# Pipelined gate eviction, an earlier first value slab, deeper look-ahead and row one-hots on two engines in a two-layer encoder

## The chip, the cores and the metric

The kernel runs on one core of a Trainium2 chip. The metric is the device time of one execution in microseconds (us). The engines are TensorE (PE, with its weight loads shown apart as PEld), VectorE (DVE), ScalarE (ACT), GpSimd (POOL) and SyncE (SP, which here only issues DMAs). Each engine takes its instructions strictly in the order of its own queue and waits on semaphores for the others.

## What is computed

Two layers, D = 1024, 256 tokens. Each layer is a mixer (a gated linear recurrence, then an RG-LRU block) followed by a product-key retrieval network over 16,384 experts, eight heads with sixteen experts each:

```python
scores = einsum('bshpd,hpkd->bshpk', q, sub_keys)
s1, i1 = top_k(scores[..., 0, :], 16);  s2, i2 = top_k(scores[..., 1, :], 16)
top_s, top_pos = top_k(s1 + s2 over all pairs, 16);  ids = i1 * 128 + i2 at top_pos
gate = softmax(top_s)
act = gelu(einsum('thkd,td->thk', u_tab[ids], h))
out = einsum('thk,thkd->td', gate * act, v_tab[ids])
```

The kernel computes the retrieval densely: every expert's activation for every token, times a 16,384 x 256 gate table that is zero where an expert was not chosen.

## The kernel before, in words

The change lies in `peer(i)` (line 1015) and its helpers; the mixers are as they were, apart from two helpers that they share. One `peer` has a query part, then two long stages.

**First stage** (64 calls of `s1`, line 1181). Slab g of `peer_u` (1 MB, 128 x 2048) is loaded by SP and taken in two half slabs. `split` (line 297) turns a half into a high and a low part: ACT copies it with rounding (line 300) into one of three buffers WS, DVE subtracts (line 301). `mm3` then runs 24 matmuls (lines 308, 309, 311). After a slab ACT takes the gelu of the result (line 1190) into the columns of A for that slab. `push` (line 279) keeps the splits `depth[0]` = 1 half slab ahead of the matmuls in program order; the buffer of a half is free again when the half three before it has been multiplied with its high part.

After every half slab `side(cost)` hands out credit to side work, which is written as generators that yield what they cost: first `routing` (top 16, softmax; credit 1.65 a half), then `gmats` (line 1192; credit 2.05 a half), which makes the gate table. It takes 32 blocks of eight tokens. `build` writes one-hot matrices on DVE: EQ of the second key index and P1, "row one-hots", of the first (both line 1204), and P2 = EQ times gate (line 1206). `mult(m)` runs four fp16 matmuls for half block m (line 1215) into two of six PSUM banks. `evict(m)` adds the high and low parts of the result: an ACT copy into the staging tile STG (line 1222, shown as xT, whose memory it uses), then a DVE add (line 1223). After a block's second half ACT issues the DMA of 512 KB that writes the block's gates to DRAM (line 1225). STG holds two blocks, so a block's first copy must wait until the DMA of the block two before it has landed.

**Second stage** (64 calls of `s2`, line 1258). For half slab j of `peer_v` a split as above; ACT copies and DVE subtracts the columns of A (lines 1296, 1297); 12 matmuls of 512 columns (line 1305) accumulate into four PSUM banks. Before A is used it is multiplied by the gates, read back from DRAM in 16 slabs of 1 MB (`gd`): `gates` (line 1245) does one DVE product of 128 x 2048 for each (line 1252), two of them right after each other for every eight value slabs. Layer 0 also reduces 24 slabs of `w_ada` here (`ada_slab`, line 394), each as two DVE instructions, after a broadcast (`row_bcast`, lines 374 and 375) of the condition; `softplus` too is side work of this stage. In layer 1 `pre_final` is.

`order` is the list of all weight slabs in the order of use. `pump` issues the next one as soon as a slot of the arena is free, and stops at a `gd` slab until the gate table is written (`tabled`). In the second half of the first stage three slots are left; the second stage gets three more at value slab 18.

Of the kernel before, what the change touches and what calls it, by code (L numbers as in the profile page):

```python
# [16 lines left out]
AF = mybir.ActivationFunctionType  # L17
# [3 lines left out]
P = 128  # L21
# [21 lines left out]
ADA_TE = 2  # L43
GLEAD = 2
GS16 = 32768.0
C_ROUTE = 1.65
C_G0 = 2.05
C_G1 = 1.45

SM = {}  # L50
# [22 lines left out]
def body(ctx, tc, A, out):  # L73
# [218 lines left out]
    def flush():  # L292
        while queue:
            run_one()
        run_posts(0)

    def split(raw):
        n = wsn[0] % NWS
        wsn[0] += 1
        ACT.activation(WS[:, n, 0], raw, AF.Copy)  # L300
        V.tensor_tensor(WS[:, n, 1], raw, WS[:, n, 0], op=OP.subtract)  # L301
        return WS[:, n, 0], WS[:, n, 1]

    def mm3(o, ws, rs, ks, start=True, stop=True):
        wh, wl = ws
# [64 lines left out]

    def row_bcast(cols, bank):

        for k in range(KD):
            V.tensor_scalar(diag[:, k % 2], ident, cols[:, k:k + 1], float(D), op0=OP.mult, op1=OP.mult)
            PE.matmul(PS[:, bank + k // 4, k % 4 * P:(k % 4 + 1) * P], ones, diag[:, k % 2], start=True, stop=True)
            if k % 2:
                yield 0.8

    cs = pool.tile([P, KD], F32, name="cond")

# [4 lines left out]
        yield from row_bcast(cs, bank)  # L385
        cond_copy(bank)

    def ada_slab():
        n, raw = take("ada")
        i, s = order[n][1:]  # L390
        for m in range(2):
            col = 2 * s + m
            r_ = raw[:, m * 1024:(m + 1) * 1024]
            V.scalar_tensor_tensor(r_, r_, 1.0, cb, op0=OP.mult, op1=OP.mult, accum_out=mod[:, i, col:col + 1])  # L394
        free(n)
        if s % 4 == 3:
            c0 = 2 * (s - 3)
            V.tensor_tensor(mod[:, i, c0:c0 + 8], mod[:, i, c0:c0 + 8],
                            sv("b_ada")[:, i * 48 + c0:i * 48 + c0 + 8], op=OP.add)
            if c0 == 40:  # L400

                V.tensor_scalar(mod[:, i, c0:c0 + 8], mod[:, i, c0:c0 + 8], 1.0 / GS16, None, op0=OP.mult)

    def weaved():
        while st["taken"] < len(order) and order[st["taken"]][0] == "ada":
            ada_slab()

    epst = pool.tile([P, 2], F32, name="eps")
    V.memset(epst, EPS)
# [604 lines left out]
    def peer(i):  # L1014
# [179 lines left out]
        def gmats():  # L1194

            P2 = pool.tile([P, 2, NTB, 2, P], F16, name="gsplit", tag="gsplit")

            def build(n):
                bf = n % 2
                ts = slice(n * NTB, (n + 1) * NTB)  # L1200
                pairs = lambda a: a.rearrange("p t (j z) -> p t j z", z=2)
                spread = lambda a: a[:, ts, None, :].to_broadcast([P, NTB, P // 2, 2])
                for dst, t_ in ((EQ, T2), (P1[:, bf], T1)):
# [13 lines left out]

            def evict(m):
                b = 2 + 2 * (m % 3)
                pv = PS[:, b:b + 2].rearrange("p a (t g j) -> p g j (a t)", t=2, g=2)  # L1220
                st_ = STG[:, m // 2 % 2, :, m % 2 * 4:m % 2 * 4 + 4]
                ACT.activation(st_, pv[:, 0], AF.Copy)  # L1222
                V.tensor_tensor(st_, pv[:, 1], st_, op=OP.add)  # L1223
                if m % 2:
                    nc.scalar.dma_start(Gd[i][:, :, m // 2],
                                        STG[:, m // 2 % 2].rearrange("p (q j) t -> p q (j t)", q=8))
# [12 lines left out]
            yield 1.0  # L1239
            for m in (S // 4 - 2, S // 4 - 1):  # L1240
                evict(m)
                yield 0.7
            tabled.add(i)
            pump()

        def gates():

            n, raw = take("gd")
            q, th = order[n][2] // 2, order[n][2] % 2
            av = slabs(aslab(16 * q), 2).rearrange("p a (j t) -> p (a j) t", t=S)[:, :, th * P:(th + 1) * P].rearrange(  # L1250
                "p j (g t) -> p j g t", t=8)
            V.tensor_tensor(av, av, raw.rearrange("p (g j t) -> p j g t", g=16, t=8), op=OP.mult)  # L1252
            free(n)

        box_wt = []
        wtn = [0]
# [1 line left out]
        def s2(cost):  # L1258
            n, raw = take("v")
            g = order[n][2]  # L1260
            if g == 63 and i == 1:
                boxes = []

# [20 lines left out]
            for half in range(2):  # L1284
# [3 lines left out]
                def prep(half=half, j=j, box=box):  # L1288
                    hi, lo = split(raw[:, half * 1024:(half + 1) * 1024])
                    if half == 1:  # L1290
                        free(n)
                    z = wtn[0] % 4
                    wtn[0] += 1
                    box["v"] = (hi, lo)
# [31 lines left out]
        if i == 0:  # L1326
            sides.append(cond)
            sides.append(softplus())
        for it in vs[i]:
            if it[0] == "ada":  # L1330
                settle(cond)
                weaved()
                continue
            if it[0] == "gd":
                gates()
                continue
            g = it[2]
            if g == 4:
                nc.sync.dma_start(XT, Xd[i])
            elif g == 18:  # L1340
                release(0, 1, 2)
            elif g == 34 and i == 0:
                release(3, 4, 5, 6, 7)
            elif g == 52 and i == 0:
                reserve(0, 1, 2, 3, 4, 5, 6)
            elif g == 58 and i == 0:
                release(13)
            s2(C_G1)
            if g == 63 and i == 1:
                flush()  # L1350
            if i == 1 and g == 44:
                sides.append(pre_final())
        if i == 0:
            release(17, 18)

# [154 lines left out]
```

## Time and profile before

| | before |
|---|---|
| median of 3 runs (range) | 2033.39 us (2030.5 to 2035.17) |
| profiled execution: its time, its span | 2030.43 us, 2028.6 us |
| mean granted TensorE clock, share of full speed | 0.986 |
| PE, PEld, DVE, ACT busy | 1943.8, 1781.8, 1571.2, 1004.0 us |
| chain that ended last | PE 88%, DVE 6%, ACT 3%, DMA 2%, issue 1% |
| HBM read and written | 418 and 37 MB |

The profile is one execution taken by the hardware profiler. A busy PE is not PE at its peak, since matmuls overlap. The chain that ended last is followed back from the last instruction, at each step to what released it. The first stage runs from about 288 to 692 us in layer 0 and from about 1244 to 1647 us in layer 1, the second from there to 1070 and to 2015 us.

### The profile page before, as it was taken

Reading aid. Unit: us, or ns where it says so; the run is one execution under the profiler, and the core shown is the slowest. Engines: PE = TensorE matmul, PEld = TensorE weight load, DVE = VectorE, ACT = ScalarE, POOL = GpSimd, SP = SyncE. Lnnn points to the kernel's source line nnn. Section 1 sums busy time; section 2 is a strip of 40 time slices with the busy share of each in tenths; the row PEclk is TensorE's granted clock in tenths of the full one; section 3 lists DMA queues with packets and bytes.
Section 4 is the critical chain, followed back from the end, with each engine's and each line's share of the span. In section 5 each row is a group of like instructions: output and inputs, shape, how many; then the busy total and the mean of one; then the engine's idle time right before and its main releaser. Section 6 shows DMA issues by size and latency. Waiting matters only on the chain.

```text
span 2028.6 us, 32101 instructions
## 1 busy us (share of the span) xinstructions
PE 1943.8 (96%) x12862; PEld 1781.8 (88%) x12862; DVE 1571.2 (77%) x2797; ACT 1004.0 (49%) x1419; POOL 0.2 (0%) x4
## 2 busy tenths in 40 slices
PE   6999999999999799999999989999999979999998
PEld 6898899999999777888888889999999978888786
DVE  6798659887888677888877776988788866676575
ACT  3544544445555354444445744445455544454454
POOL 0000000000000000000000000000000000000000
PEclk9999999999999899999999999999999989999999
DMA  8654714455767667989753482545676766766561
GB/s 347 271 200 163 285 69 158 175 187 198 238 193 244 210 247 269 394 347 399 290 208 154 158 306 90 185 167 192 208 244 195 235 225 261 290 252 260 203 234 57
DMA packets 125765, 456.87 MB, mean 225 GB/s; under 512 B 7720, under 2 KB 73512, under 8 KB 74672
## 3 DMA queue, kind: packets, MB, share of 16 engines
q1 hardware_dynamic: 59056, 421.28, 55.4%
q10 hardware_dynamic: 66560, 33.56, 5.5%
q8 instruction: 100, 1.64, 0.3%
q14 instruction: 49, 0.40, 0.1%
HBM read 418.10 MB, written 36.70 MB: 224 GB/s over the span
## 4 chain that ended last, share of the span: by engine, by line
PE 88%; DVE 6%; ACT 3%; DMA 2%; issue 1%; SPq 0%; DVEq 0%; ACTq 0%
PE psum L1305 33%; PE psum L311 14%; PE psum L308 14%; PE psum L309 14%; PE psum L1215 3%; PE psum L478 2%; DVE wsplit L301 1%; PE psum L358 1%; DMA arena<-peer_v_dram 1%; PE psum L688 1%; PE psum L318 1%; PE psum L595 1%; ACT wsplit L300 1%; PE psum L1088 1%; PE psum L915 1%
## 5 line engine op out<-in xcount | busy, mean ns | idle before, releaser
L301 DVE TENSOR_TENSOR wsplit<-arena,wsplit 128x1024 fp32r<-128x1024 f32 x600 | 729.7, 1219 | 300.8 <-ACT wsplit L300 298.4
L300 ACT ACTIVATE wsplit<-arena 128x1024 fp32r<-128x1024 f32 x600 | 632.4, 1056 | 492.1 <-PE psum L1305 311.4
L1305 PE MATMUL psum<-wsplit,gsplit 128*128 128x512 f32 x3048 | 703.3, 392 | 19.4 <-ACT gsplit L1296 14.3
L1305 PEld LDWEIGHTS psum<-wsplit,gsplit 128*128 128x128 f32 x3048 | 574.8, 189 | 145.3 <-ACT gsplit L1296 15.4
L308 PE MATMUL psum<-hsplit,wsplit 128*128 128x256 f32 x2448 | 607.7, 286 | 2.1 <-ACT wsplit L300 2.1
L309 PE MATMUL psum<-hsplit,wsplit 128*128 128x256 f32 x2448 | 600.5, 283 | 0.0
L308 PEld LDWEIGHTS psum<-hsplit,wsplit 128*128 128x128 f32 x2448 | 469.1, 192 | 4.3 <-ACT wsplit L300 2.7
L309 PEld LDWEIGHTS psum<-hsplit,wsplit 128*128 128x128 f32 x2448 | 469.6, 192 | 0.1
L311 PE MATMUL psum<-hsplit,wsplit 128*128 128x256 f32 x2448 | 344.2, 283 | 2.7 <-DVE wsplit L301 2.7
L311 PEld LDWEIGHTS psum<-hsplit,wsplit 128*128 128x128 f32 x2448 | 316.5, 192 | 3.1 <-DVE wsplit L301 3.1
L1190 ACT ACTIVATE arena<-psum 128x512 f32<-128x512 f32 x128 | 76.5, 598 | 283.2 <-PE psum L311 283.2
L1223 DVE TENSOR_TENSOR xT<-psum,xT 128x512 f32<-128x512 f32 x128 | 87.6, 686 | 51.9 <-ACT xT L1222 51.9
L1297 DVE TENSOR_TENSOR gsplit<-arena,gsplit 128x256 fp32r<-128x256 f32 x254 | 105.9, 417 | 0.0
L1296 ACT ACTIVATE gsplit<-arena 128x256 fp32r<-128x256 f32 x254 | 101.4, 399 | 0.0
L394 DVE SCALAR_TENSOR_TENSOR arena<-arena,scratch 128x1024 f32<-128x1024 f32 x80 | 94.1, 1218 | 0.0
L1252 DVE TENSOR_TENSOR arena<-arena 128x2048 f32<-128x2048 f32 x32 | 71.9, 2284 | 12.2 <-DMA arena<-gates 12.2
L1222 ACT ACTIVATE xT<-psum 128x512 f32<-128x512 f32 x128 | 75.1, 589 | 8.1 <-PE psum L1215 8.1
L1206 DVE TENSOR_TENSOR gsplit<-scratch 128x2048 f16<-128x2048 f16 x64 | 78.0, 1218 | 0.0
L1215 PE MATMUL psum<-gsplit,scratch 128*128 128x256 f16 x512 | 67.0, 274 | 0.0
L1215 PEld LDWEIGHTS <-scratch 128*128 128x128 f16 x512 | 44.9, 98 | 7.1
L697 DVE TENSOR_TENSOR arena<-arena 128x512 f32<-128x512 f32 x56 | 35.7, 683 | 12.0 <-PE psum L688 6.8
L1204 DVE TENSOR_TENSOR scratch<-iota,T 128x1024 f16<-128x1024 f16 x64 | 43.8, 684 | 0.0
(219 smaller groups left out, 1258.5 us busy)
## 6 DMA issues: line engine op xcount, KB each, us to landing
arena<-peer_u_dram SPq DMA_DIRECT2D x128, 1024.0 KB, 4.9
arena<-peer_v_dram SPq DMA_DIRECT2D x128, 1024.0 KB, 4.9
arena<-w_ada_dram SPq DMA_DIRECT2D x40, 1024.0 KB, 5.9
gates<-xT ACTq DMA_DIRECT2D x64, 512.0 KB, 5.3
arena<-gates SPq DMA_DIRECT2D x32, 1024.0 KB, 4.7
arena<-w_q_dram SPq DMA_DIRECT2D x16, 1024.0 KB, 6.9
arena<-hg_k_dram SPq DMA_DIRECT2D x8, 1024.0 KB, 15.5
arena<-hg_s_dram SPq DMA_DIRECT2D x8, 1024.0 KB, 6.1
```

Of the source, the lines that this page charges most:

```text
L300: ACT.activation(WS[:, n, 0], raw, AF.Copy)
L301: V.tensor_tensor(WS[:, n, 1], raw, WS[:, n, 0], op=OP.subtract)
L308: PE.matmul(o, wh(k), rh(k), start=start and k == 0, stop=False)
L309: PE.matmul(o, wh(k), rl(k), start=False, stop=False)
L311: PE.matmul(o, wl(k), rh(k), start=False, stop=stop and k == ks - 1)
L394: V.scalar_tensor_tensor(r_, r_, 1.0, cb, op0=OP.mult, op1=OP.mult, accum_out=mod[:, i, col:col + 1])
L1206: V.tensor_tensor(P2[:, bf].rearrange("p t g (j z) -> p t g j z", z=2), pairs(EQ)[:, :, None].to_broadcast([P, NTB, 2, P // 2, 2]), TG[:, ...
L1215: PE.matmul(PS[:, b + t // 2, t % 2 * S:(t % 2 + 1) * S], P1[:, n % 2, 4 * h + t], P2[:, n % 2, 4 * h + t], start=True, stop=True)
L1223: V.tensor_tensor(st_, pv[:, 1], st_, op=OP.add)
L1296: ACT.activation(box_wt[0][:, z, 0], acol(j), AF.Copy)
L1297: V.tensor_tensor(box_wt[0][:, z, 1], acol(j), box_wt[0][:, z, 0], op=OP.subtract)
L1305: PE.matmul(PS[:, 4 + 2 * tb + dh], box_wt[0][:, z, a, tb * P:(tb + 1) * P], r[:, dh * 512:(dh + 1) * 512], start=(j == 0 and a == 0 and r ...
```

## The change

1. `evict` becomes `step(m)`, one per half block. It issues the DMA of a finished block (half block m-3 is its second), then the ACT copy of half block m-1, the DVE add of m-2, and the matmuls of m.
2. In 11 of the 32 blocks (n % 3 == 1) ACT makes the row one-hots: eight Abs of 128 x 128 with a bias column, then one Relu over 128 x 1024; DVE then makes only EQ and P2.
3. The credit of a half slab rises (1.65 to 1.7, 2.05 to 2.2); a block yields 2.7 + 0.7 + 0.7 as before, or 2.0 + 0.7 + 0.7 where ACT makes its one-hots.
4. In the second stage the splits run two half slabs ahead (`depth[0] = 2`), with five buffers: H, idle there, lends two (`widen`). Value slab 0 stands ahead of the first two gate slabs in `order`.
5. The gate products are cut into quarters of a pair (128 x 1024) and handed out one per half slab (`between`), as are the halves of an `ada` slab. Arena slots are released one by one from value slab 5 on; the broadcast of the condition starts at slab 4, softplus at slab 20.

```diff
-C_ROUTE = 1.65
-C_G0 = 2.05
+C_ROUTE = 1.7
+C_G0 = 2.2
...
-                    if max(0, 8 * q - GLEAD) == it[2]:
+                    if q and 8 * q - GLEAD == it[2]:
                         zs += [("gd", i, 2 * q), ("gd", i, 2 * q + 1)]
             zs.append(it)
+            if it[0] == "v" and it[2] == 0:
+                zs += [("gd", i, 0), ("gd", i, 1)]
...
     def split(raw):
-        n = wsn[0] % NWS
+        hs = homes[-1]
+        w_ = hs[wsn[0] % len(hs)]
...
+    def between():
+        for xs in (steps_gate, steps_ada):
+            if xs:
+                xs.pop(0)()
+                return
...
+            def by_act(n):
+                return n % 3 == 1
+
+            def row_onehots(n, part):
+
+                if not by_act(n) or n >= S // NTB:
+                    return
+                if part == 2:
+                    ACT.activation(P1[:, n % 2], P1[:, n % 2], AF.Relu, scale=-1.0, bias=1.0)
+                    return
+                for t in range(4 * part, 4 * part + 4):
+                    ACT.activation(P1[:, n % 2, t], io1, AF.Abs, scale=-1.0, bias=T1[:, n * NTB + t, 0:1])
...
-            def evict(m):
-                b = 2 + 2 * (m % 3)
...
-                ACT.activation(st_, pv[:, 0], AF.Copy)
-                V.tensor_tensor(st_, pv[:, 1], st_, op=OP.add)
-                if m % 2:
-                    nc.scalar.dma_start(Gd[i][:, :, m // 2],
...
+            def step(m):
+
+                if m - 3 >= 0 and (m - 3) % 2:
+                    n = (m - 3) // 2
+                    nc.scalar.dma_start(Gd[i][:, :, n], STG[:, n % 2].rearrange("p (q j) t -> p q (j t)", q=8))
+                if 0 <= m - 1 < S // 4:
+                    pv, st_ = view(m - 1)
+                    ACT.activation(st_, pv[:, 0], AF.Copy)
+                if 0 <= m - 2 < S // 4:
+                    pv, st_ = view(m - 2)
+                    V.tensor_tensor(st_, pv[:, 1], st_, op=OP.add)
+                if m < S // 4:
+                    mult(m)
 
             for n in range(S // NTB):
                 build(n)
-                yield 2.7
-                if n:
-                    evict(2 * n - 2)
-                    yield 0.7
-                mult(2 * n)
-                if n:
-                    evict(2 * n - 1)
-                    yield 0.7
-                mult(2 * n + 1)
...
+                row_onehots(n + 1, 0)
+                yield 2.0 if by_act(n) else 2.7
+                step(2 * n)
+                row_onehots(n + 1, 1)
                 yield 0.7
+                step(2 * n + 1)
+                row_onehots(n + 1, 2)
+                yield 0.7
...
+            for z in range(2):
+                for th in range(2):
+                    steps_gate.append(lambda z=z, th=th: part(z, th))
...
+        depth[0] = 2
+        widen([H[:, n].rearrange("p k t -> p (k t)").rearrange("p (a x) -> p a x", a=2) for n in range(2)])
```

Two places show how rows move. The first is ACT's queue in layer 0's first stage, with the semaphores that a row waits for (DMAHW is a DMA's). Before, around one block (L1190 gelu, L1222 copy of a half block, L1225 the block's DMA, L300 split):

```order
L1222 ACTIVATE xT<-psum 128x128x4
L1225 DMA gates<-xT 1024x1x128 [waits DVE_49]
L300 ACTIVATE wsplit<-arena 128x1024 [waits DMAHW1_49,Activation_49]
L1222 ACTIVATE xT<-psum 128x128x4 [waits DMAHW5_49,PE_49]
L300 ACTIVATE wsplit<-arena 128x1024 [waits Activation_49]
L1190 ACTIVATE arena<-psum 128x512 [waits PE_49]
```

Now, around one block (L1225 is now the gelu, L1275 the block's DMA, L1278 the copy, L317 the split):

```order
L1275 DMA gates<-xT 1024x1x128 [waits DVE_49]
L1278 ACTIVATE xT<-psum 128x128x4 [waits PE_49]
L1278 ACTIVATE xT<-psum 128x128x4 [waits DMAHW0_49,PE_49]
L317 ACTIVATE wsplit<-arena 128x1024
L1225 ACTIVATE arena<-psum 128x512
L317 ACTIVATE wsplit<-arena 128x1024 [waits DMAHW2_49,Activation_49]
```

In both, the copy that waits for a DMA writes the staging buffer of the block two before its own. Before, that block's DMA stands one block further up in the queue: the DMA shown in the fence is the next one. Now `step(2N)` issues the DMA of block N-2, and `step(2N+1)` brings the copy of half block 2N that waits for it: the DMA is the one shown, one copy above.

The second place is DVE's queue where layer 0's second stage begins. Before (L301 split, L1223 add, L1252 gate product, L1297 A's low part, L374 broadcast):

```order
L301 TENSOR_TENSOR wsplit<-arena,wsplit 128x1024
L1223 TENSOR_TENSOR xT<-psum,xT 128x128x4 x3
L1252 TENSOR_TENSOR arena<-arena 128x16x128 x2
L301 TENSOR_TENSOR wsplit<-arena,wsplit 128x1024
L1297 TENSOR_TENSOR gsplit<-arena,gsplit 128x256
L374 TENSOR_SCALAR scratch<-consts,cond 128x128 x6
```

Now (L318 split, L1281 add, L1310 quarter product, L1366 A's low part):

```order
L1281 TENSOR_TENSOR xT<-psum,xT 128x128x4 x2
L318 TENSOR_TENSOR wsplit<-arena,wsplit 128x1024 x10
L1310 TENSOR_TENSOR arena<-arena 128x8x128 x2
L1366 TENSOR_TENSOR gsplit<-arena,gsplit 128x256
L318 TENSOR_TENSOR wsplit<-arena,wsplit 128x1024
L1310 TENSOR_TENSOR arena<-arena 128x8x128
```

Before, the last adds of the gate table stand right ahead of the first gate products; now ten splits lie between them, and the broadcast has left this place.

## Rows read from the trace of the kernel before

**Rows 1.** The page: PE busy in tenths, 40 slices of the span.
```profile
PE   6999999999999799999999989999999979999998
```

**Rows 2.** Stretches of 20 us: busy PE, PEld, DVE, ACT, POOL; clock, DMA share, GB/s.
```profile
300.00:320.00 20.00, 20.00 (x169) 20.00 (x168) 20.00 (x90) 8.26 (x10) 0.00 (x0) 1.00 0.38 137
...
600.00:620.00 20.00, 20.00 (x171) 19.63 (x170) 17.69 (x22) 10.84 (x16) 0.00 (x0) 1.00 0.73 238
...
680.00:700.00 20.00, 12.46 (x106) 12.01 (x104) 10.66 (x12) 4.99 (x8) 0.00 (x0) 0.87 0.49 161
700.00:720.00 20.00, 13.71 (x56) 10.61 (x56) 11.01 (x26) 10.85 (x17) 0.00 (x0) 0.79 0.46 182
...
920.00:940.00 20.00, 19.06 (x85) 15.41 (x84) 18.45 (x24) 9.26 (x15) 0.00 (x0) 1.00 1.01 422
...
1640.00:1660.00 20.00, 9.10 (x68) 8.52 (x68) 9.68 (x10) 5.00 (x9) 0.00 (x0) 0.76 0.62 229
```

**Rows 3.** Chain of work that ended last, pieces: start us, us, what.
```profile
249.70 0.96 PE psum L311 x8
252.58 0.96 PE psum L311 x8
...
688.71 0.47 PE psum L1215 x4
...
689.83 1.30 DVE xT L1223 x2
691.15 3.47 DMA gates<-xT
...
695.17 6.69 DMA arena<-peer_v_dram
```

**Rows 4.** Timeline of ACT in layer 0's first stage: start us, us, instruction, idle before.
```profile
559.83 0.60 ACT L1190 ACTIVATE arena<-psum 128x512 f32<-128x512 f32 x1 [1.68 <-PE psum L311]
560.33 0.59 ACT L1222 ACTIVATE xT<-psum 128x512 f32<-128x512 f32 x1
561.67 0.52 ACTq L1225 DMA_DIRECT2D gates<-xT  x1
562.30 1.06 ACT L300 ACTIVATE wsplit<-arena 128x1024 fp32r<-128x1024 f32 x1 [1.38 <-DVE scratch L1204]
563.26 0.58 ACT L1222 ACTIVATE xT<-psum 128x512 f32<-128x512 f32 x1
563.74 1.05 ACT L300 ACTIVATE wsplit<-arena 128x1024 fp32r<-128x1024 f32 x1
...
568.31 0.52 ACTq L1225 DMA_DIRECT2D gates<-xT  x1
```

**Rows 5.** The chain of work that ended last, later pieces.
```profile
882.52 42.95 PE psum L1305 x188
...
1016.87 53.16 PE psum L1305 x233
...
1643.94 0.47 PE psum L1215 x4
...
2015.01 1.37 PE psum L1278 x6
```

**Rows 6.** Groups of instructions: count, busy us and mean ns, idle before.
```profile
L1296 ACT ACTIVATE gsplit<-arena 128x256 fp32r<-128x256 f32 x254 | 101.4, 399 | 0.0
...
L1252 DVE TENSOR_TENSOR arena<-arena 128x2048 f32<-128x2048 f32 x32 | 71.9, 2284 | 12.2 <-DMA arena<-gates 12.2
...
L926 ACT ACTIVATE arena<-psum,smalls 128x256 f32<-128x256 f32 x32 | 13.0, 476 | 2.8 <-PE psum L915 2.8
```

**Rows 7.** DMA issues: count, size each, median us to landing.
```profile
arena<-gates SPq DMA_DIRECT2D x32, 1024.0 KB, 4.7
```

**Rows 8.** Line 1225 from 500 to 685 us: the gate write's issue to its landing.
```profile
DMA to landing us min/median/max: 3.5/5.3/6.8
```

More of the change, by code (lines that the diff above doesn't have):

```diff
@@ L295, in flush, with widen, narrow @@
         run_posts(0)
+    homes = [[WS[:, n] for n in range(NWS)]]
+    kept = []
+    def widen(more):
+        n = wsn[0]
+        homes.append([homes[0][(n + z) % NWS] for z in range(NWS)] + more)
+        kept.append(n)
+        wsn[0] = 0
+    def narrow():
+        homes.pop()
+        wsn[0] = kept.pop()
     def split(raw):
-        n = wsn[0] % NWS
+        hs = homes[-1]
+        w_ = hs[wsn[0] % len(hs)]
         wsn[0] += 1
-        ACT.activation(WS[:, n, 0], raw, AF.Copy)
-        V.tensor_tensor(WS[:, n, 1], raw, WS[:, n, 0], op=OP.subtract)
-        return WS[:, n, 0], WS[:, n, 1]
+        ACT.activation(w_[:, 0], raw, AF.Copy)
+        V.tensor_tensor(w_[:, 1], raw, w_[:, 0], op=OP.subtract)
+        return w_[:, 0], w_[:, 1]
     def mm3(o, ws, rs, ks, start=True, stop=True):
@@ L371, in row_bcast @@
     def row_bcast(cols, bank):
[L373 to L377, printed above, removed]
+        for k in range(0, KD, 2):
+            for z in range(2):
+                V.tensor_scalar(diag[:, z], ident, cols[:, k + z:k + z + 1], float(D), op0=OP.mult, op1=OP.mult)
+            yield 0.8
+            for z in range(2):
+                PE.matmul(PS[:, bank + k // 4, (k + z) % 4 * P:((k + z) % 4 + 1) * P], ones, diag[:, z], start=True,
+                          stop=True)
+            yield 0.1
     cs = pool.tile([P, KD], F32, name="cond")
@@ L386, in load_cond, with ada_parts, ada_part @@
         cond_copy(bank)
-    def ada_slab():
+    def ada_parts():
         n, raw = take("ada")
+        return [lambda m=m: ada_part(n, raw, m) for m in range(2)]
+    def ada_part(n, raw, m):
         i, s = order[n][1:]
[L391 to L394, printed above, removed]
+        col = 2 * s + m
+        r_ = raw[:, m * 1024:(m + 1) * 1024]
+        V.scalar_tensor_tensor(r_, r_, 1.0, cb, op0=OP.mult, op1=OP.mult, accum_out=mod[:, i, col:col + 1])
+        if m == 0:
+            return
         free(n)
@@ L405, in weaved @@
         while st["taken"] < len(order) and order[st["taken"]][0] == "ada":
-            ada_slab()
+            for f in ada_parts():
+                f()
+    steps_ada, steps_gate = [], []
+    def between():
[3 more added lines that the diff above has]
+                return
     epst = pool.tile([P, 2], F32, name="eps")
@@ L1246, in gates, with part @@
         def gates():
[L1248 to L1253, printed above, removed]
+            two = [take("gd"), take("gd")]
+            def part(z, th):
+                n, raw = two[th]
+                q = order[n][2] // 2
+                av = slab(aslab(16 * q + 8 * z)).rearrange("p (j t) -> p j t", t=S)[:, :, th * P:(th + 1) * P].rearrange(
+                    "p j (g t) -> p j g t", t=8)
+                V.tensor_tensor(av, av, raw.rearrange("p (g j t) -> p j g t", g=16, t=8)[:, 8 * z:8 * z + 8], op=OP.mult)
+                if z == 1:
+                    free(n)
+            for z in range(2):
+                for th in range(2):
+                    steps_gate.append(lambda z=z, th=th: part(z, th))
         box_wt = []
@@ L1260, in s2 @@
             g = order[n][2]
+            while g % 8 == 0 and g and steps_gate:
+                steps_gate.pop(0)()
             if g == 63 and i == 1:
@@ L1291, in prep @@
                         free(n)
+                    if j == 0:
+                        gates()
+                        between()
+                    between()
                     z = wtn[0] % 4
@@ L1339, in peer @@
                 nc.sync.dma_start(XT, Xd[i])
[L1340 to L1344, printed above, removed]
+                if i == 0:
+                    sides.append(cond)
+            if g == 20 and i == 0:
+                sides.append(softplus())
+            if g % 4 == 1 and g > 4:
+                z = g // 4 - 1
+                if z in ((0, 1, 2, 3, 4, 5, 6, 7) if i == 0 else (0, 1, 2, 7)):
+                    release(z)
+            if g == 52 and i == 0:
                 reserve(0, 1, 2, 3, 4, 5, 6)
@@ L1347, in peer @@
                 release(13)
+            if g == 63:
+                depth[0] = 1
             s2(C_G1)
@@ L1352, in peer @@
                 sides.append(pre_final())
+        narrow()
+        while steps_ada:
+            steps_ada.pop(0)()
         if i == 0:
```

25 lines of the change are left out of this document (12 added, 13 removed).

## The prediction, made before the change was run

> **What bounds the kernel now.** I read the page first, then the table of 20 us stretches, the chain that ended last, and the timelines of ACT and DVE. The page's slices show PE busy almost everywhere, with dips at the ends of the stages [rows 1]. In the first stage PE never stops: 20.00 of 20 us at full clock, with DVE at 17.69 and ACT at 10.84 [rows 2]. So nothing that only frees DVE there can save time; it can only cost. A half slab takes PE 2.88 us, the distance of two groups of eight low-part matmuls [rows 3], and a block of eight fp16 matmuls 6.64 - 2 x 2.88 = 0.88 us, where 6.64 us is the distance of two gate writes [rows 4].
>
> The time that can be won lies in the second stage. In layer 0 the last fp16 matmul ends at 689.18 us [rows 3], one half slab of 2.88 us follows it, and the second stage ends at 1070.03 us [rows 5]: 378.0 us. Its 1524 matmuls at 42.95/188 = 0.2285 us are 348.2 us [rows 5]. That leaves 29.8 us. Layer 1's, counted the same way, runs from 1647.29 to 2015.01 us: 367.7 us, 19.5 us over [rows 5]. The chain says what the gap at the start is: last add, gate write 3.47 us, then value slab 0 behind two gate slabs, 6.69 us [rows 3]. The clock falls there too, to 0.87 and 0.79 of full speed, 0.76 in layer 1 [rows 2]. A smaller, repeated loss is the pair of gate products, 2 x 2.28 us of DVE at once [rows 6], after which PE misses 0.94 us in a stretch [rows 2].
>
> **The second stage: a gain.** The credits now end the gate table about ten half slabs before the first stage does (counted in the built order of PE's queue: the last fp16 group stands 11 half slabs before the first matmul of the second stage; before, one). The write and the wait for it thus lie beside 29 us of matmuls, and value slab 0 no longer queues behind the gate slabs. The gate product in quarters costs DVE the same sum, some 1.14 us a time, beside matmuls; two half slabs of look-ahead cover that. The condition's broadcast and layer 1's transposes stay on PE: 48 small matmuls, by four in 0.47 us [rows 3] up to twice as long, 6 to 11 us. Of 29.8 + 19.5 = 49.3 us at most some 41 can go. Something stays at the start: the arena has three slots there, the second gate slab waits for the last `peer_u` slab's slot, needs 4.7 us to land [rows 7] and two quarter products before value half 0 can be multiplied. I put this at 6 us a layer, clock included, an estimate. **Gain: 41 - 12 = 29 us**, between 8 (little more than the 0.94 us gaps, of which there are five) and 41.
>
> **The first stage: a new wait on ACT.** Taking 11 one-hots of 128 x 1024 from DVE, and its wait for the ACT copy, gains nothing: PE is full there. What the eviction as a pipeline adds decides. Before, a block's first copy waits for a gate write that was issued more than a block earlier, over 6.64 us, against 5.3 us to land (3.5 to 6.8) [rows 4, 8]: the wait is over when ACT gets there. Now that write is issued one copy ahead of the copy that waits for it. ACT works in order, so it stands until the write has landed, and all splits queue behind it. With three WS buffers ACT cannot be far ahead of PE: a buffer is free when two thirds of the half slab three before are done, and the split takes 1.06 us [rows 4], so its lead is at most 2 x 2.88 + 0.96 - 1.06 = 5.7 us; I take 5.
>
> In the built order of layer 0 there are 30 such waits. Between a waiting copy and the next gate write, ACT's queue holds in all 30 copies, 42 splits, 21 gelus, 40 Abs and 10 Relu; only the rest (30 copies, 10 splits, 5 gelus, 40 Abs) lies beside a landing. From start to start a copy takes 0.48, a split 0.96, a gelu 0.50 us [rows 4]; a Relu of the split's size 0.96. An Abs does not occur before: 0.399 us for 256 columns [rows 6] less 0.10 for 128 of them (512 take 0.60 [rows 4]), plus 0.08 for a bias column (0.476 against 0.399 [rows 6], the nearest row), less the 0.10 by which neighbours overlap: 0.28, between 0.20 and 0.38. The sum is 14.4 + 40.3 + 10.5 + 11.2 + 9.6 = 86.0 us. ACT's queue therefore needs 30 L + 86.0 us, where L is the time from issue to landing. In the same stretch PE needs 52 half slabs and 30 blocks: 52 x 2.88 + 30 x 0.88 = 176.2 us. What ACT needs more, less its lead, is a stall of PE.
>
> L is 3.5 us with nothing beside it [rows 3, 8] and 5.3 us at the median, where a `peer_u` slab is in flight. Now 26 slabs fall on the 30 writes, and a slab is issued when its second split is done, close to the next write, sometimes just behind it. I take 4.7, nearer to 5.3. Then ACT needs 227.0 us, 50.8 more than PE, and **a layer loses 45.8 us, two layers 92 us**. At 3.5 it is 9.8 us a layer, 20 in all; at 5.3 it is 63.8, 128 in all.
>
> The trace's 3.5 us for 512 KB on idle DMA engines is the floor of L. [...]
>
> The rest is costed at nothing. Splitting eight fp16 matmuls into four and four: the blocks' period shows no price for the change of type beyond the 0.88 us. The higher routing credit: DVE is full in the routing's bursts, 20.00 of 20, with PE also at 20.00 [rows 2]; 0.05 more credit over some 60 half slabs is about 3 us of work moved forward, cover enough if spread, up to 3 us a layer if not. DVE's waits behind ACT are hidden as long as ACT is the later of the two. XT's reload at value slab 4 stays where it was. ACT's queue still carries the gate writes' issue, 0.52 us, within L.
>
> **Sum.** +92 - 29 = +63 us on the profiled execution's 2030.4 us, 2093; its runs' median is 3.0 us above it, so 2033.4 + 63 = **2096 us**. A measurement of this kernel can tell about 0.2%, 4 us, from no change.
>
> **Rivals.**
> 1. *The landing is short (faster).* The writes land as if alone, because PE's and so the slabs' pace falls and they seldom meet. For it: 3.5 us does occur. Against: 26 slabs for 30 writes, and 5.3 at the median with the same mix. At 3.5 us: +20 - 29 gives 2024 us; without any stall 2004 us. The point from which it decides: 2 x (30 L + 86.0 - 176.2 - 5) = 29, L = 3.66 us. Chance 0.14. [...]
> 2. *The landing is a little above that.* L from 3.66 to 4.1 us gives 0 to +27 us, 2033 to 2060 us. [...] Chance 0.12, a third of it within 0.2%.
> 3. *The writes collide fully.* In the slowed rhythm slab and write are issued at the same moment, in every block, and L is 6 us (6.8 occurs [rows 8]): +170 - 29, 2174 us. PE's many short stops could lower its clock as well, as in the stretches at 0.79 and 0.87 [rows 2]; against that, 920 to 940 us has a stop and a clock of 1.00. Chance 0.12.
> 4. *The second stage's gain stays out*, because DVE, at 18.45 of 20 us in layer 0 [rows 2], cannot run ahead: then, with layer 0's 20 us lost, +83 instead of +63, 2116 us. This lies inside the forecast's range.
>
> **How the numbers follow.** The forecast, L between 4.1 and 5.5 us, has 0.62: 55.6 to 139.6 us of stalls, with the gain of 29 2060 to 2144 us, and some 10 us more on either side for the gain's own bounds. Rivals 1, 2 and 3 have 0.14, 0.12 and 0.12. Faster is rival 1; the same is a third of rival 2, 0.04; slower is the rest, 0.82. The range that leaves out 2 in 10 goes from 2022 us (half of rival 1 lies below it) to 2155 us (rival 3 lies above it).
>
> **What would show it.** Right: in the first stages PE below 16 of 20 us while the gate table is made; ACT copies of the eviction with idle time of 2 to 4 us before them, released by the gate write; splits released late, so that PE waits for ACT's split. A gap of under 6 us at the start of the second stage, where before value slab 0 landed only at 701.9 us [rows 3], 9.8 us after the first stage's end, and hardly any 0.94 us gaps. Wrong: PE still at 20.00 of 20 in the first stage, or the waiting copies released by PE rather than by the DMA. If the landings are near 3.5 us, rival 1 holds; if ACT's idle time before the copies is short although landings are long, the lead was larger than I took it for.

## The result, and the profile after

The changed kernel takes 2041.07 us (median of 10 runs, 2035.7 to 2048.71) against 2031.78 us of before in the same comparison: a ratio of 1.0051, 95% interval 1.0033 to 1.0069. It is slower, as forecast, but by some 10 us and not by 63. The two profiled executions have spans of 2044.0 and 2028.6 us, 15.4 us apart.

Three lines of the page after, the slices of PE and the chain that ended last:

```profile
PE   6999999999999999999999899999899999999998
...
PE 74%; DVE 10%; DMA 7%; ACT 7%; issue 2%; ACTq 0%; SPq 0%; DVEq 0%
PE psum L1374 33%; PE psum L325 10%; PE psum L326 10%; PE psum L328 10%; DMA gates<-xT 6%; DVE wsplit L318 3%; ACT wsplit L317 2%; PE psum L513 2%; PE psum L375 1%; PE psum L723 1%; PE psum L335 1%; PE psum L1263 1%; DVE arena L581 1%; ACT xT L1278 1%; DVE xT L1281 1%
```

The two slices with a 7 of before [rows 1] are gone, and the gate write (gates<-xT) is now on the chain with 6% of the span. Stretches of 20 us say where PE lost time instead (columns as in [rows 2]):

```profile
480.00:500.00 20.00, 17.60 (x138) 17.08 (x136) 15.44 (x18) 12.95 (x23) 0.00 (x0) 0.91 0.56 185
...
540.00:560.00 20.00, 17.48 (x145) 16.57 (x143) 15.11 (x18) 13.07 (x24) 0.00 (x0) 1.00 0.72 223
...
580.00:600.00 20.00, 20.00 (x171) 19.55 (x171) 17.00 (x20) 12.62 (x24) 0.00 (x0) 1.00 0.44 135
...
1460.00:1480.00 20.00, 17.89 (x139) 17.33 (x138) 13.62 (x16) 12.59 (x23) 0.00 (x0) 0.91 0.60 193
...
1500.00:1520.00 20.00, 16.59 (x136) 15.57 (x135) 15.16 (x19) 13.26 (x24) 0.00 (x0) 1.00 0.57 179
```

While the gate table is made PE is busy for 16.6 to 20.0 of 20 us, where it had 20.00 before [rows 2]. The granted clock, 1.00 before in all of both first stages, now falls in stretches in which PE stops, or right behind one: 0.91 from 480 to 500 us in layer 0, and in layer 1 0.93, 0.98 and 0.91 in the three stretches from 1420 to 1480 us and 0.91 from 1540 to 1560. A clock of 0.91 in 20 us is worth at most 1.8 us of PE, so this is at most 1.8 us of layer 0's loss and 5.4 us of layer 1's (an estimate from these rows). Measured from the first matmul with the keys (lines 1088 and 1123) to the end of the first stage, which is now also the start of the second, the stages were 401.3 and 401.2 us long and are now 419.4 and 429.5: +18.1 and +28.3 us. The second stage's matmuls, in each layer (line 1374, count, ns, first and last start):

```profile
L1374 PEld LDWEIGHTS psum<-wsplit,gsplit x936: 186/188/333, 712.1 to 1068.8; 128*128 128x128 f32 x188
...
L1374 PEld LDWEIGHTS psum<-wsplit,gsplit x912: 186/188/333, 1674.0 to 2029.8; 128*128 128x128 f32 x183
```

They begin as soon as the first stage ends and take 356.7 and 355.8 us. Before it was 378.0 us from the first stage's end (692.1) to the last such start, and 367.1 in layer 1. That is a gain of 21.3 + 11.3 = 32.6 us against a loss of 46.4 us. The remaining 1.6 us of the 15.4 lie outside these stages. At the start of the second stage PE now waits once for a split, 2.63 us, and once for 0.35:

```profile
712.13 5.80 PE L1374 MATMUL psum<-wsplit,gsplit 128*128 128x512 f32 x24
720.56 2.07 PE L1374 MATMUL psum<-wsplit,gsplit 128*128 128x512 f32 x4 [2.63 <-ACT gsplit L1365]
722.99 3.78 PE L1374 MATMUL psum<-wsplit,gsplit 128*128 128x512 f32 x8 [0.35 <-DVE gsplit L1366]
```

From 760 to 1060 us PE is busy for 300.00 of 300 us. The waits in layer 0's first stage, 476 to 715 us (engine, what waited and for whom, us, times, longest):

```profile
DVE wsplit L318 <- ACT wsplit L317: 49.5, 33, 5.2
ACT xT L1278 <- DMA gates<-xT: 37.8, 17, 5.6
ACT xT L1278 <- PE psum L1263: 25.1, 13, 3.5
...
PEld L1263 <- issue: 13.3, 12, 2.5
PE psum L1263 <- DVE xT L1281: 8.2, 8, 1.5
...
PE psum L325 <- ACT wsplit L317: 1.8, 3, 1.2
```

The eviction's copy (L1278) does wait for the gate write, but in only 17 of 30 blocks. Thirteen copies wait for PE, for the fp16 group that they are to evict: nine of them are copies that also needed the write, which had landed by then, and four are others. In both layers together it is 34 waits of 82.9 us and 26 of 52.8. PE in turn stands mostly ahead of an fp16 group (L1263) and seldom ahead of a half slab. For 8.2 us there the profile names DVE's add, which frees the PSUM banks, for 3.3 us DVE's P2 (a line left out here), and for 13.3 us of the weight loads no cause. The landing of the write, of line 1275:

```profile
DMA to landing us min/median/max: 3.5/4.1/8.1
```

One long landing on ACT's timeline (columns as in [rows 4]):

```profile
535.34 1.05 ACT L317 ACTIVATE wsplit<-arena 128x1024 fp32r<-128x1024 f32 x1
536.10 0.52 ACTq L1275 DMA_DIRECT2D gates<-xT  x1
536.29 1.05 ACT L317 ACTIVATE wsplit<-arena 128x1024 fp32r<-128x1024 f32 x1
537.24 0.58 ACT L1225 ACTIVATE arena<-psum 128x512 f32<-128x512 f32 x1
...
540.06 0.60 ACT L1278 ACTIVATE xT<-psum 128x512 f32<-128x512 f32 x1 [0.60 <-PE psum L1263]
540.11 0.52 ACTq L1275 DMA_DIRECT2D gates<-xT  x1
540.56 1.05 ACT L1241 ACTIVATE scratch<-scratch 128x1024 f16<-128x1024 f16 x1
541.50 1.05 ACT L317 ACTIVATE wsplit<-arena 128x1024 fp32r<-128x1024 f32 x1
...
545.69 0.60 ACT L1278 ACTIVATE xT<-psum 128x512 f32<-128x512 f32 x1 [1.22 <-DMA gates<-xT]
546.17 0.52 ACTq L1275 DMA_DIRECT2D gates<-xT  x1
546.18 1.05 ACT L317 ACTIVATE wsplit<-arena 128x1024 fp32r<-128x1024 f32 x1
547.14 0.60 ACT L1278 ACTIVATE xT<-psum 128x512 f32<-128x512 f32 x1
553.35 0.60 ACT L1278 ACTIVATE xT<-psum 128x512 f32<-128x512 f32 x1 [5.61 <-DMA gates<-xT]
553.63 0.52 ACTq L1275 DMA_DIRECT2D gates<-xT  x1
553.84 1.05 ACT L317 ACTIVATE wsplit<-arena 128x1024 fp32r<-128x1024 f32 x1
554.79 0.59 ACT L1225 ACTIVATE arena<-psum 128x512 f32<-128x512 f32 x1
555.26 1.27 ACT L1244 ACTIVATE scratch<-iota,T 128x128 f16<-128x128 f16 x4
556.44 1.05 ACT L317 ACTIVATE wsplit<-arena 128x1024 fp32r<-128x1024 f32 x1
557.38 0.58 ACT L1278 ACTIVATE xT<-psum 128x512 f32<-128x512 f32 x1
```

A `peer_u` slab was issued at 545.57, the write at 546.17; it lands after 7.1 us, and ACT stands for 5.61 us. The split after it ends late, and on PE's timeline that costs 1.20 us:

```profile
554.94 0.39 PE L325 MATMUL psum<-hsplit,wsplit 128*128 128x256 f32 x1 [1.20 <-ACT wsplit L317]
```

ACT's lead covered the rest. So a stand of ACT is not a stop of PE of the same length; what each is worth had to be measured.

### The profile page after: what moved, and what is told of

Read it like the earlier page. It is cut to its first block, busy times and chain, and to the rows that moved or that the text cites. A ratio compares the mean times of both kernels' runs of the same rounds, so it can differ in the third digit from the quotient of the medians.

```text
span 2044.0 us, 32275 instructions
## 1 busy us (share of the span) xinstructions
PE 1953.3 (96%) x12862; PEld 1788.1 (87%) x12862; DVE 1575.4 (77%) x2807; ACT 1073.9 (53%) x1617; POOL 0.2 (0%) x4
## 4 chain that ended last, share of the span: by engine, by line
PE 74%; DVE 10%; DMA 7%; ACT 7%; issue 2%; ACTq 0%; SPq 0%; DVEq 0%
PE psum L1374 33%; PE psum L325 10%; PE psum L326 10%; PE psum L328 10%; DMA gates<-xT 6%; DVE wsplit L318 3%; ACT wsplit L317 2%; PE psum L513 2%; PE psum L375 1%; PE psum L723 1%; PE psum L335 1%; PE psum L1263 1%; DVE arena L581 1%; ACT xT L1278 1%; DVE xT L1281 1%
## 5 line engine op out<-in xcount | busy, mean ns | idle before, releaser
L318 DVE TENSOR_TENSOR wsplit<-arena,wsplit 128x1024 fp32r<-128x1024 f32 x500 | 607.4, 1220 | 277.1 <-ACT wsplit L317 274.3
L317 ACT ACTIVATE wsplit<-arena 128x1024 fp32r<-128x1024 f32 x500 | 522.7, 1050 | 86.0 <-PE psum L326 35.6
L1374 PE MATMUL psum<-wsplit,gsplit 128*128 128x512 f32 x1848 | 434.3, 393 | 6.5 <-ACT gsplit L1365 5.2
L1374 PEld LDWEIGHTS psum<-wsplit,gsplit 128*128 128x128 f32 x1848 | 348.6, 189 | 81.4 <-ACT gsplit L1365 6.1
L1374 PE MATMUL psum<-hsplit,gsplit 128*128 128x512 f32 x1200 | 282.1, 391 | 0.0
L1374 PEld LDWEIGHTS psum<-hsplit,gsplit 128*128 128x128 f32 x1200 | 226.1, 189 | 47.1
L1225 ACT ACTIVATE arena<-psum 128x512 f32<-128x512 f32 x128 | 76.0, 594 | 203.5 <-PE psum L328 203.5
L1366 DVE TENSOR_TENSOR gsplit<-arena,gsplit 128x256 fp32r<-128x256 f32 x254 | 107.0, 421 | 60.8 <-ACT gsplit L1365 60.8
L1278 ACT ACTIVATE xT<-psum 128x512 f32<-128x512 f32 x128 | 76.2, 596 | 137.5 <-DMA gates<-xT 82.9
L318 DVE TENSOR_TENSOR hsplit<-arena,hsplit 128x1024 fp32r<-128x1024 f32 x100 | 122.3, 1223 | 26.5 <-ACT hsplit L317 25.8
L317 ACT ACTIVATE hsplit<-arena 128x1024 fp32r<-128x1024 f32 x100 | 104.6, 1046 | 7.9 <-DMA arena<-peer_v_dram 7.9
L1263 PE MATMUL psum<-gsplit,scratch 128*128 128x256 f16 x512 | 74.8, 276 | 23.1 <-DVE xT L1281 16.4
L1281 DVE TENSOR_TENSOR xT<-psum,xT 128x512 f32<-128x512 f32 x128 | 83.9, 681 | 0.0
```

The lines of the kernel that those rows point to most:

```text
L317: ACT.activation(w_[:, 0], raw, AF.Copy)
L318: V.tensor_tensor(w_[:, 1], raw, w_[:, 0], op=OP.subtract)
L1366: V.tensor_tensor(box_wt[0][:, z, 1], acol(j), box_wt[0][:, z, 0], op=OP.subtract)
L1374: PE.matmul(PS[:, 4 + 2 * tb + dh], box_wt[0][:, z, a, tb * P:(tb + 1) * P], r[:, dh * 512:(dh + 1) * 512], start=(j == 0 and a == 0 and r ...
```

## The experiments

Each was run beside the kernel before on the same chip. "First stage" is the time from the first key matmul to the first matmul of the second stage, in layers 0 and 1; before, some 16 and 11 us of it were the gap at the start of the second stage. Two runs that stood beside different runs of the kernel before are best compared by their ratios, times 2032 us.

| run | us | ratio to before, 95% interval | first stage |
|---|---|---|---|
| before | 2031.8 | 1 | 417.3, 412.5 |
| the change | 2041.1 | 1.0051 (1.0033 to 1.0069) | 419.4, 429.5 |
| 1 third buffer | 2020.6 | 0.9940 (0.9927 to 0.9953) | 411.4, 411.6 |
| 2 early write | 2049.7 | 1.0086 (1.0072 to 1.0101) | 426.9, 431.2 |
| 3 one-hots on DVE | 2013.5 | 0.9908 (0.9893 to 0.9922) | 409.1, 409.8 |
| 4 old eviction, one-hots on DVE | 2006.4 | 0.9871 (0.9856 to 0.9886) | 405.4, 405.4 |
| 5 third buffer, one-hots on DVE | 2006.1 | 0.9884 (0.9869 to 0.9899) | 404.8, 404.8 |
| 6 third buffer, later copies | 2001.2 | 0.9857 (0.9842 to 0.9872) | 403.0, 402.9 |
| 7 old eviction, one-hots on ACT | 2034.3 | 1.0018 (1.0009 to 1.0028) | 418.6, 418.6 |
| 8 as 4, old credits | 2014.6 | 0.9921 (0.9908 to 0.9935) | 410.2, 410.2 |
| 9 as 6, one-hots on DVE | 2000.0 | 0.9834 (0.9820 to 0.9847) | 401.8, 401.8 |
| 10 as 6, gate slabs first | 2006.4 | 0.9865 (0.9850 to 0.9881) | 405.8, 406.0 |
| 11 as 6, one half slab ahead | 2001.1 | 0.9840 (0.9827 to 0.9854) | 403.0, 402.9 |
| 12 as 6, whole gate products | 2000.8 | 0.9838 (0.9825 to 0.9851) | 403.0, 402.9 |

**1. A third buffer.** Nothing in the order of instructions changes; the copy waits for a write issued over a block earlier.

```diff
+            def stg(n):
+                if n % 3 < 2:
+                    return STG[:, n % 3]
...
+                    third[n] = (slab(13)[:, 0:1024] if g < 49 else slab(18)[:, 1024:2048]).rearrange(
+                        "p (j t) -> p j t", t=NTB)
...
-                    nc.scalar.dma_start(Gd[i][:, :, n], STG[:, n % 2].rearrange("p (q j) t -> p q (j t)", q=8))
+                    nc.scalar.dma_start(Gd[i][:, :, n], stg(n).rearrange("p (q j) t -> p q (j t)", q=8))
```

> The changed kernel with a third block buffer for the table's eviction, in free columns of the arena; the order of all instructions stays, only the copy of a block now waits for the gate write of three blocks before, not two. Theory A (the first stage's loss comes from ACT standing at the copy until the write just issued has landed): the 34 waits of 83 us of ACT go, and with them nearly all of the 18 + 28 us that the two first stages are longer than before; 2041 - 46 = 1995 us, 1995 to 2008. Rival B (PE loses its time at the fp16 groups because copy, add and one-hots follow each other too closely, and the writes only fill time that ACT had anyway): 2030 to 2041 us, with the waits of the copies for PE grown.

Measured 2020.6 us, half way between the two theories. All waits for the write are gone from the copy (its line in this run, both layers), and waits for PE have doubled from 52.8 us:

```profile
  PE psum L1263: 104.6, 62
```

Standing for the write cost 2041.1 - 2020.6 = 20 us in both layers, 23 by the ratios. Some 20 us were still lost.

**2. The write a half block earlier**, issued by ACT right behind the block's last add.

```diff
-                if m - 3 >= 0 and (m - 3) % 2:
-                    n = (m - 3) // 2
-                    nc.scalar.dma_start(Gd[i][:, :, n], STG[:, n % 2].rearrange("p (q j) t -> p q (j t)", q=8))
...
                     V.tensor_tensor(st_, pv[:, 1], st_, op=OP.add)
+                    if m % 2:
+                        n = (m - 2) // 2
+                        nc.scalar.dma_start(Gd[i][:, :, n], STG[:, n % 2].rearrange("p (q j) t -> p q (j t)", q=8))
```

> The changed kernel with the gate write issued right behind the block's last add, a half block earlier and ahead of the next block's one-hots; two buffers as before. Theory A: between the write and the copy that needs its buffer lies a whole block again, so the copy hardly waits; ACT waits for the add instead, under 1 us a block and mostly hidden: 1995 to 2012 us. Rival B: 2030 us or more. Rival C (waiting for DVE's add is as long a stand as waiting for the landing, since DVE is 16 to 19 of 20 us busy there): 2025 to 2050 us.

Measured 2049.7 us, 8.6 us more than the change. That lies in the ranges of rivals B and C; the waits from 476 to 720 us speak for C:

```profile
ACT xT L1275 <- PE psum L1263: 22.4, 14, 2.5
ACT xT L1275 <- DMA gates<-xT: 20.5, 12, 4.7
...
ACT wsplit L317 <- DVE scratch L1252: 8.1, 6, 2.0
ACT scratch L1244 <- DVE scratch L1252: 7.7, 6, 2.2
ACT scratch L1241 <- DVE scratch L1252: 7.4, 6, 2.0
ACT wsplit L317 <- DVE xT L1278: 6.8, 4, 2.6
```

(Line 1275 is the copy here, 1278 the add.) The waits for the write fell from 37.8 to 20.5 us, but ACT now stands 30 us for DVE: the issue of the write needs the add, and whatever follows it in ACT's queue, splits and one-hots, is shown as waiting for DVE.

**3 and 4. One-hots back on DVE; and the whole eviction of before besides.** Run 3 changes one line; run 4 puts the whole of `gmats` back as it was, and keeps the credits and the second stage of the change.

```diff
-                return n % 3 == 1
+                return False
```

```diff
-            def step(m):
...
+            def evict(m):
...
+                ACT.activation(st_, pv[:, 0], AF.Copy)
+                V.tensor_tensor(st_, pv[:, 1], st_, op=OP.add)
+                if m % 2:
+                    nc.scalar.dma_start(Gd[i][:, :, m // 2],
+                                        STG[:, m // 2 % 2].rearrange("p (q j) t -> p q (j t)", q=8))
```

> The changed kernel with all row one-hots on DVE again; the copies still wait for the write just issued. Theory A: ACT has no Abs and Relu between the waits, 20.8 us less a layer, and the blocks stand further apart, so that 30 x 4.1 + 65 us of ACT hardly exceed PE's work; most of the 46 us goes: 2000 to 2015 us. Rival B: the one-hots on ACT are what keeps DVE from being late at 2.2 us of credit, so without them PE waits for DVE: 2041 us or more. If the landing wait alone counts, whatever else ACT does: no change, 2035 to 2045 us.

> The changed kernel with the table's part alone put back (one-hots on DVE, copy, add and write of a half block together, as before); the credits and the whole second stage as changed. If the second stage's gain of 31 us stands on its own and the first stage runs as before: 2032 - 31 = 2001 us, 1997 to 2008. Rival: at 2.2 us of credit the table runs denser than DVE can follow (17.7 of 20 us before), and PE waits in the first stage: 2012 to 2030 us.

Run 3 measured 2013.5 us, with 34 waits of 85 us for the write left. Without Abs and Relu on ACT waits as long as the change's cost PE much less, though not nothing (the table at the end of this section). Run 4 measured 2006.4 us, near the 2001 expected: its first stages lose 4 us each.

**5 and 6. What is left of the loss: the copies' wait for PE.** Run 5 is run 1 with the one-hots on DVE. Run 6 is run 1 with the copy one step later:

```diff
-                if 0 <= m - 1 < S // 4:
-                    pv, st_ = view(m - 1)
-                    ACT.activation(st_, pv[:, 0], AF.Copy)
                 if 0 <= m - 2 < S // 4:
                     pv, st_ = view(m - 2)
+                    ACT.activation(st_, pv[:, 0], AF.Copy)
                     V.tensor_tensor(st_, pv[:, 1], st_, op=OP.add)
```

> Third block buffer and all row one-hots on DVE; what stays of the changed eviction is that a half block's copy follows its multiplication by one step. In the run with the third buffer alone 62 copies wait for PE's fp16 group, 105 us of ACT, and it is 20 us above the 2000 us hoped for; with the one-hots on DVE and the old buffers 34 waits for writes (85 us) cost hardly anything (2013 against 2006 us). Theory D (a wait of ACT costs PE only where ACT has the Abs and Relu to do as well; each wait alone is covered): 2003 to 2010 us. Rival E (the copies' waits for PE cost by themselves): 2013 to 2022 us.

> Third block buffer, one-hots of every third block on ACT, and the copy of a half block one step later (together with its add), so that it waits neither for a write nor for the fp16 group just issued. Theory D or E (the copies' waits for PE, 105 us of ACT with the third buffer alone, are what is left of the loss): 2003 to 2010 us, and ACT's idle time before the copies under 20 us. Rival F (the Abs and Relu themselves delay the splits, 3.4 us of ACT and PE's wait for the Relu in every third block, whatever the copies do): 2016 to 2022 us, as with the third buffer alone.

Measured 2006.1 us, in theory D's range, and 2001.2, just below the range of D or E. In run 6 the copies wait hardly at all (their line, both layers):

```profile
  PE psum L1263: 5.5, 9
  DVE scratch L1252: 5.3, 5
```

and PE has 20.00 of 20 us in most stretches although ACT makes every third block's one-hots. From run 1 to run 6 it is 0.9940 to 0.9857, 17 us: the price of copying a half block one step behind its multiplication. This settles rival F: the one-hots alone do not cost it. Run 5 looks from the other side: 64 such waits, 149 us of ACT, cost less where ACT has no one-hots, 6 to 10 us (run 9 has neither).

**7. One-hots on ACT with the old eviction.** The old eviction, in which the write's issue waits on ACT for DVE's add, with `row_onehots` as changed (against the change):

```diff
                 row_onehots(n + 1, 0)
                 yield 2.0 if by_act(n) else 2.7
-                step(2 * n)
+                if n:
+                    evict(2 * n - 2)
+                    yield 0.7
+                mult(2 * n)
                 row_onehots(n + 1, 1)
...
```

> The run with the table's old eviction (2006 us), with the row one-hots of every third block on ACT. Theory D: with no wait of the pipeline ACT has time for them: 2003 to 2010 us. Rival F: the one-hots on ACT cost by themselves, 2014 us or more. Rival C: here the write's issue waits on ACT for DVE's add, as in the run with the early write (2050 us), so ACT's work comes in bursts behind DVE: 2015 to 2040 us.

Measured 2034.3 us: 28 us above run 4, 30 by the ratios. It lies in the ranges of rivals F and C; run 6 has ruled out F, which leaves C. The waits from 476 to 720 us:

```profile
ACT wsplit L317 <- DVE xT L1271: 29.3, 13, 4.2
ACT scratch L1244 <- DVE scratch L1252: 16.7, 6, 4.1
ACT wsplit L317 <- DVE scratch L1252: 14.0, 6, 2.7
```

So by the ratios the same one-hots cost 30 us beside a wait for DVE's add, 29 beside the change's waits (the change against run 3), 11 beside the copies' waits alone (run 1 against 5), and at most some 5 beside none (runs 6 and 9, which are not told apart: the intervals meet at 0.9842 to 0.9847).

**8. The credits of before, with the old eviction.**

```diff
-C_ROUTE = 1.7
-C_G0 = 2.2
+C_ROUTE = 1.65
+C_G0 = 2.05
```

> The run with the table's old eviction (2006 us), with the credits of before (1.65 and 2.05), so that the table ends one half slab before the stage does instead of seven. If the early end is what brings the second stage's gain: the last write and the gate slabs come late, and of the start's gaps (some 20 us in the two layers) most are back, less the 10 us that the first stages lose at 2.2 us of credit: 2008 to 2018 us, first stage of layer 0 ending at 692 to 693 us instead of 697. If value slab 0 ahead of the table is enough: 1996 to 2002 us.

Measured 2014.6 us, in the range for "the early end brings it". From 690 to 710 us:

```profile
PEld psum L1354 <- ACT gsplit L1345: 10.1, 2, 8.7
PE psum L1354 <- ACT gsplit L1345: 9.4, 2, 8.5
ACT gsplit L1345 <- DVE arena L1290: 7.7, 1, 7.7
...
DVE arena L1290 <- DMA arena<-gates: 4.0, 1, 4.0
```

The first stage itself is back at 401.4 us, but the second begins 8.5 us late: the gate product waits for its gate slab, which needs the last write. Before, PE waited 12.5 us there.

**9 to 12. Parts of the change, undone one at a time in run 6.** In the order of runs 9, 10, 11 and 12:

```diff
-                return n % 3 == 1
+                return False
...
-                    if q and 8 * q - GLEAD == it[2]:
+                    if max(0, 8 * q - GLEAD) == it[2]:
...
-            if it[0] == "v" and it[2] == 0:
-                zs += [("gd", i, 0), ("gd", i, 1)]
...
-        depth[0] = 2
+        depth[0] = 1
...
                     if j == 0:
                         gates()
+                    while steps_gate:
                         between()
                     between()
```

> The run with third buffer and later copies (2001 us), with all row one-hots on DVE. If the one-hots on ACT bring something once ACT waits for nothing: DVE is late at 2.2 us of credit and the first stages lose some 3 to 5 us each, as with the old eviction (692 to 697 us in layer 0): 2004 to 2010 us. If DVE has room without them: 1999 to 2003 us.

> The run with third buffer and later copies (2001 us), with the first two gate slabs ahead of value slab 0 again. If the early end of the table is what closes the gap at the start: both gate slabs and value slab 0 have landed in time either way, 2000 to 2004 us. If the order of the loads does: value slab 0 comes two slabs later, some 4 to 6 us a layer, 2008 to 2014 us.

> The run with third buffer and later copies (2001 us), with one half slab ahead in the second stage instead of two (the five split buffers stay). If the look-ahead covers the gate products: the 0.94 us gaps come back, up to some 14 of them, and some of the start's gap: 2006 to 2016 us. If the products in quarters are enough: 2000 to 2004 us.

> The run with third buffer and later copies (2001 us), with the four quarter products of a gate pair at once, some 4.6 us of DVE, two half slabs ahead as changed. If two half slabs of PE (5.5 us) cover them: 2000 to 2004 us. If DVE's splits behind them come late: a gap of 1 to 2 us at each of 14 pairs, 2010 to 2028 us.

Run 9, 2000.0 us: DVE has room without help. Run 10, 2006.4 us: between its two cases; the order of the loads is worth 2.8 and 3.1 us a layer (second stages that begin at 405.8 and 406.0 instead of 403.0 and 402.9), the rest comes from the early end. Runs 11 and 12, 2001.1 and 2000.8 us: neither the second half slab of look-ahead nor the quartered product is needed as long as the other is there. Both undone together was not tried.

Runs 6, 9, 11 and 12 beat both kernels, by 1.4 to 1.7% against before. The simplest of them, run 9, needs neither one-hots on ACT nor a copy close behind its matmuls, only the raised credits, the third buffer, one step between a half block's eviction and its write, and the second stage of the change.

Six of the kernels make a table of the two waits and the one-hots, as ratios to before:

| ACT's copies wait for | one-hots on ACT | one-hots on DVE |
|---|---|---|
| the write just issued, and PE | 1.0051 (the change) | 0.9908 (run 3) |
| PE alone | 0.9940 (run 1) | 0.9884 (run 5) |
| hardly anything | 0.9857 (run 6) | 0.9834 (run 9) |

With the one-hots on ACT the wait for the write costs 23 us and the wait for PE 17; without them 5 (not clear of noise: the intervals of runs 3 and 5 overlap) and 10. The first stages of the profiled executions give 26 and 17, 9 and 6. So theory D holds in the main: a wait costs far more where ACT has the one-hots as well. That each wait alone is covered goes too far, since both together still cost 15 us without the one-hots.

## Why the prediction was right or wrong

**The second stage, right.** Forecast 29 us, measured 32.6; where the first stage is nearly undisturbed, run 6, the whole kernel is 29 us faster (0.9857). The early end, which the prediction names first, is worth 8.5 us a layer (run 8); the 6 us a layer put down for the start were 3.0 us of waits and a stretch of 20 us at a granted clock of 0.83. The 0.94 us gaps went. That DVE's relief is worth nothing was right too (run 9).

**The first stage, right in its sign and in one of its causes, wrong in size.** It was to lose 92 us and lost 46.4 in the profiled execution, some 40 by the ratios (the change against run 6); PE fell below the 16 of 20 us that had been named as a sign in no stretch of 20 us. The step that failed is "Between a waiting copy and the next gate write, ACT's queue holds in all 30 copies, 42 splits, 21 gelus, 40 Abs and 10 Relu", and with it 86.0 us and the 92 us. That is the order in the queue. In the trace 45 of the 64 writes do not wait until ACT has worked off what stands ahead of them. This is the built order of ACT's queue for the writes of 529.28, 536.10 and 540.11 us, to set beside the timeline above:

```
L1275 DMA gates<-xT 1024x1x128
L1278 ACTIVATE xT<-psum 128x128x4 x2
L1244 ACTIVATE scratch<-iota_82,T_81 128x128 x4
L317 ACTIVATE wsplit<-arena 128x1024 x2
L1225 ACTIVATE arena<-psum 128x512
L1275 DMA gates<-xT 1024x1x128
L1278 ACTIVATE xT<-psum 128x128x4
L1244 ACTIVATE scratch<-iota_82,T_81 128x128 x4
L1278 ACTIVATE xT<-psum 128x128x4
L1241 ACTIVATE scratch<-scratch 128x1024
L317 ACTIVATE wsplit<-arena 128x1024
L1275 DMA gates<-xT 1024x1x128
```

The second write stands behind two splits and a gelu, and was issued at 536.10, ahead of the second split (536.29) and the gelu (537.24). In layer 0's trace 33 splits, 21 gelus, 60 Abs and 5 Relu lie between a write's issue and the copy that waits for it, where the queue's order has 10, 5, 40 and none. So only 30 copies, 19 splits, 5 gelus, 20 Abs and 5 Relu lie outside a landing: 14.4 + 18.2 + 2.5 + 5.6 + 4.8 = 45.5 us at the same prices, not 86.0. The prices held: four Abs take 1.17 us from start to start, 0.29 each against 0.28.

**L, too high.** 4.1 us at the median, not 4.7; that alone would have made 27.8 us a layer of the forecast's 45.8. With both corrected the sum is 30 x 4.1 + 45.5 = 168.5 us of ACT for 176 of PE, and would give no loss at all. So the sign came out right partly by luck: the sum as it was meant finds no loss, and the wait for the write still cost 20 us or more (run 1). The likely reason is the spread, which a sum over medians does not see: landings up to 8.1 us and stands up to 6.5, where 5 us of lead were assumed. That is argued, not shown; how the loss divides over the single waits was not measured. In the profiled executions run 1 also has two stretches at a clock of 0.91 fewer, which is up to 3.6 us of the difference.

**A term that was missing.** "The rest is costed at nothing" took in that a half block's copy now follows its multiplication by one step. Where both steps of a block fall behind the same half slab, ACT stands until PE has reached that fp16 group, and only then makes its next split. I had named this only as a sign that the forecast would be wrong. It was 26 copies of 128 in the change, 62 in run 1, and is worth 17 us there (run 1 against 6). DVE seems to hand it on: in run 1 it idles 47.7 us in layer 0 for ACT's splits (32.0 in run 6), and 3.8 us of PE's waits are put down to DVE's adds; the rest of that path is argued.

**The rivals.** Rival 2's outcome came true (2033 to 2060 us), with its landing of 4.1 us at the upper edge, but by two causes of 23 and 17 us, not by its one. Run 1 does the same work with the wait one block later and is 1.1% faster than the change. No write landed in less than the 3.5 us that the prediction took as the floor. Run 2 shows what an earlier issue can cost: there it has to wait for DVE's add, and ACT stands 30 us for DVE in layer 0.

## What to carry to other kernels

On an engine that works in order, as ACT's 1584 activations did here, look for every wait that a reordering creates, for a write just issued, for the matmul just issued, and for another engine's result ahead of a DMA issue; the first two cost 15 us together here while the one-hots were on DVE, and some 40 once ACT made them too. Give a buffer or a step of distance before moving work there. And count what hides a DMA from issue times in a trace of the same queue, not from the order alone.

## What the runs showed of the hardware

In the trace of the changed kernel ACT issues a DMA ahead of activations that precede it in its queue, when what the DMA needs is done (each of the 64 writes was issued 0.03 us or more after the end of the add that it needs): at 540.11 us, 0.05 us after a copy began, the write was issued that stands behind a Relu (540.56) and a split (541.50) in the built order. At 553.63 us it went ahead of seven: a split, a gelu, four Abs and a split stand between it and the copy of 557.38, which follows it directly in the built order. This sets right the sentence at the top that each engine takes its instructions strictly in the order of its own queue: in the kernel before ACT did, and each of its 64 writes was issued 0.03 us after its add; in the changed kernel its 1584 activations began in the built order, but not the DMAs that it issues. In layer 0 this moved 23 splits, 16 gelus, 20 Abs and 5 Relu from before a landing into it, over 30 blocks. The opposite holds when the DMA has to wait: then the work behind it stands as well, up to 4.2 us for a split in run 7.

Of the 64 writes in the changed kernel 45 went ahead of one to seven activations, and none ahead of more than seven. No run tests whether there is a limit.
